# Depthwise convolution of a hybrid decoder: three channel tiles on PE with tables laid out beforehand, two running sums on DVE

## The chip, the cores and the metric

One core of one Trainium2 chip. The metric is the device time of one execution in microseconds (us); lower is better. Of a kernel's runs the median is given.

## The reference

A two-layer decoder trunk over 2048 tokens of 1024 channels, float32. Layer 0 mixes pooling and a state space model. Layer 1, which the change is about, is a gated causal depthwise convolution of width 31, a LayerNorm over channels and an output projection. Cut to that layer:

```python
def _odd_mixer(h, w_in, conv_w, conv_b, ln_g, ln_b, w_out):
    proj = jnp.einsum('bsd,de->bse', h, w_in)
    val, gt, z = ...                      # 1024 channels each
    g = (val * jax.nn.sigmoid(gt)).astype(jnp.float32)
    c = lax.conv_general_dilated(g, conv_w[:, None, :], window_strides=(1,),
        padding=[(30, 0)], feature_group_count=1024) + conv_b
    cc = c - jnp.mean(c, axis=-1, keepdims=True)
    var = jnp.mean(cc * cc, axis=-1, keepdims=True)
    c = cc * lax.rsqrt(var + LN_EPS) * ln_g + ln_b
    y = jax.nn.silu(c) * jax.nn.silu(z)
    return jnp.einsum('bse,ed->bsd', y, w_out)
# x = x + _odd_mixer(_rmsnorm(x), ...); the output is _rmsnorm(x)
```

## The kernel before

The tokens are worked on in two halves of 1024, A and B (`h` = 0 and 1), and each half in two blocks of 512 (`b`). Channels lie in eight tiles `j` of 128. Projections run on PE (TensorE) as three products of split float32 operands, 48 products of 512 columns a unit; a weight is fetched as `raw` and split into a high and a low part `w` by ACT (ScalarE) and DVE (VectorE) ("weight split"; its DVE row is `w<-raw,w`, or `act<-raw,act` for the last four).

Nothing is ordered by hand. Each part of the work is a generator that yields operations; a scheduler (`Sched.run`) merges these streams into one order per engine before anything runs, by estimated engine clocks, and a stream of a lower number (`prio`) goes first among those about as early. Engines then work through their queues in that order. PE's main stream takes the units in this order: layer 0 of A and of B, layer 0's output of A, layer 1's projections of A, layer 0's output of B, layer 1's projections of B, then the output projection of A (`A.q`, eight units `e{eh}t{tp}`: half of the output channels by 256 tokens) and that of B (`B.q`, eight units, all of block 0 first, then block 1).

The projections of layer 1 take, for each channel tile in `ORDER[h]`, gate `g{j}` and value `v{j}`, and then the eight `y{j}`. `post_val` multiplies them and stores the tile to DRAM, for the convolution on DVE into `gd`, for that on PE into `gpd`.

*Convolution on DVE*: `conv_load` brings the tile into a `cg` slot and starts the accumulator `ca` on ACT with tap 0. `conv_thread`, the stream of lowest priority (9), adds the other 30 taps one after the other into that accumulator (`SCALAR_TENSOR_TENSOR ca<-cg,cwt,ca`). The last two tiles go block by block, first both for block 0, then both for block 1. `conv_store` writes the sum to `cd`. *Convolution on PE*: `pe_conv` multiplies tables of shifted taps with eight channels by 16 token phases at a time. `pe_tables` and ACT (with `mask8`) build the tables on the chip. Tiles 6 and 7 (`PEB`) go through PE for both halves together, in products of 128 columns; tiles 4 and 5 only for half B, in products of 64. All of this happens in layer 1 of B. DVE has tiles 0 to 5 of A and 0 to 3 of B.

`ln_thread(h, b)` waits for all eight tiles of `cd` of a block and loads them (`act<-cd`, or `ca<-cd` and `cg<-cd` for B's block 1). It adds them up on DVE to a half sum of 512 columns and lets PE form the mean (`aux<-st,onesN`), subtracts it (`act<-act,aux`), squares on ACT and adds up to a second half sum, lets PE form the variance (`aux<-onesN,st`), takes the inverse root on POOL, spreads it with PE (`aux<-st,ones`) and multiplies. `ln_out` applies gain, SiLU and the gate and splits the result into `y1`, which the output projection reads.

`evac1` empties a finished output unit on DVE, 512 columns twice (`st<-st,mm`); for the second half of the channels, ACT squares, POOL takes a root and DVE multiplies by it and by the norm's gain (`st<-st,sml,act`, here called output norm).

## Time and profile before

| what | us |
|---|---|
| median of 3 runs | 1534.59 (1533.71 to 1536.25) |
| span of the profiled execution | 1533.6 |
| PE busy | 1493.4 |
| DVE busy | 1090.1 |
| ACT busy | 549.5 |
| PE idle in 1400 to 1480 | 3.25 |
| last evacuation of A's output projection, start | 1432.79 |

The profile is of one execution; no other time is given for it than its span, from the first to the last instruction, which lies 1.0 us below the median of the runs. A row of a group reads: line, engine, operation, tile written and tiles read, shape, count, then busy time, mean ns of one, idle time of the engine before it and what ended that. A row of the timeline has start, length and the count of equal instructions that it merges; a row of a window has the length, then the busy time of PE, PEld (weight load), DVE, ACT, POOL, the granted clock, and the DMA's share and GB/s.

### The profile page before, as it was taken

How to read it: one execution, taken by the hardware profiler on the slowest of the kernel's cores; microseconds unless marked ns; L12 is line 12 of the kernel's file. 1: busy time of each engine (PE TensorE's matmuls, PEld its weight loads, DVE VectorE, ACT ScalarE, POOL GpSimd, SP SyncE). 2: the span in 40 equal slices, each digit the busy share in tenths (PEclk: the TensorE clock that was granted, in tenths of full speed). 3: DMA queues.
4: the chain of work that ended last, by engine and by line, in shares of the span. 5: the costliest groups of instructions: out<-in, count | busy, mean ns of one | idle time of the engine just before them, and what ended most of it. 6: DMA issues, size and time to landing. Idle time of an engine off the chain costs nothing. (4 is left out here: it accounts for less than half of the span.)

```text
span 1533.6 us, 18686 instructions
## 1 busy us (share of the span) xinstructions
PE 1493.4 (97%) x7087; PEld 1224.7 (80%) x7087; DVE 1090.1 (71%) x1291; ACT 549.5 (36%) x859; POOL 124.2 (8%) x397
## 2 busy tenths in 40 slices
PE   5999999999999999999999999999999999999997
PEld 4878788888887788888888888888888888887785
DVE  5891567778857323399999999344997898967752
ACT  5322463222134215311111430352354565533431
POOL 4000121000000002000000000120000000003322
PEclk9999999999999999999999999999999999999999
DMA  6227973889665544233353543633466585966753
GB/s 193 83 86 234 313 238 116 255 266 332 221 222 194 168 165 137 83 97 95 98 97 112 191 144 118 218 98 111 88 148 202 160 248 188 354 217 226 246 200 115
DMA packets 248618, 271.35 MB, mean 177 GB/s; under 512 B 58497, under 2 KB 178993, under 8 KB 248528
## 3 DMA queue, kind: packets, MB, share of 16 engines
q1 hardware_dynamic: 248528, 270.15, 55.6%
q8 instruction: 56, 0.92, 0.2%
q14 instruction: 34, 0.28, 0.1%
HBM read 174.49 MB, written 91.42 MB: 173 GB/s over the span
## 5 line engine op out<-in xcount | busy, mean ns | idle before, releaser
L348 PE MATMUL mm<-act,w 128*128 128x512 f32 x4224 | 1004.9, 396 | 0.0
L348 PEld LDWEIGHTS mm<-act,w 128*128 128x128 f32 x4224 | 789.0, 189 | 178.2 <-issue 2.5
L305 DVE SCALAR_TENSOR_TENSOR ca<-cg,cwt,ca 128x1024 f32<-128x1024 f32 (+1 forms) x360 | 397.8, 1106 | 16.1 <-ACT ca L330 5.8
L348 PE MATMUL mm<-w,act 128*128 128x512 f32 x1344 | 316.6, 395 | 1.4 <-DVE w L287 1.4
L348 PEld LDWEIGHTS mm<-w,act 128*128 128x128 f32 x1344 | 251.7, 188 | 60.4 <-DVE w L287 1.8
L287 DVE TENSOR_TENSOR w<-raw,w 128x1024 fp32r<-128x1024 f32 x116 | 141.6, 1222 | 104.3 <-ACT w L319 101.8
L319 ACT CAST w<-raw 128x1024 fp32r<-128x1024 f32 x116 | 121.2, 1045 | 195.6 <-PE mm L348 152.1
L330 ACT ACTIVATE junk<-st 128x1024 bf16<-128x1024 f32 (+1 forms) x64 | 54.0, 844 | 121.3 <-DVE st L287 111.8
L305 DVE SCALAR_TENSOR_TENSOR act<-aux,vcol,act 128x512 fp32r<-128x512 f32 x64 | 45.9, 748 | 66.1 <-ACT act L330 66.0
L287 DVE TENSOR_TENSOR st<-st,mm 128x512 f32<-128x512 f32 x48 | 31.0, 684 | 74.7 <-PE mm L348 74.5
L330 ACT ACTIVATE po<-mm 128x1024 f32<-128x1024 f32 x32 | 32.9, 1027 | 119.8 <-PE mm L348 79.2
L319 ACT CAST act<-st 128x512 fp32r<-128x512 f32 (+1 forms) x64 | 51.8, 860 | 59.1 <-DMA st<-y0d 16.2
L297 POOL TENSOR_SCALAR sml<-sml 128x1 f32<-128x1 f32 (+1 forms) x100 | 34.4, 344 | 430.8 <-ACT junk L330 423.5
L319 ACT COPY st<-aux 128x512 f32<-128x512 f32 (+2 forms) x56 | 25.7, 474 | 114.9 <-PE aux L348 99.7
L330 ACT ACTIVATE act<-act,mask 128x128 f32<-128x128 f32 x192 | 58.0, 390 | 19.4 <-DMA act<-band 19.4
L521 POOL TENSOR_TENSOR sml<-sml,mhalf 128x1 f32<-128x1 f32 (+1 forms) x52 | 34.4, 662 | 346.2 <-DVE sml L295 342.2
L287 DVE TENSOR_TENSOR act<-st,act 128x512 fp32r<-128x512 f32 (+1 forms) x64 | 56.2, 926 | 8.3 <-ACT act L319 8.3
L330 ACT ACTIVATE act<-aux,vcol 128x512 fp32r<-128x512 f32 x64 | 41.6, 686 | 47.6 <-PE aux L362 47.5
L362 PE MATMUL aux<-ident,st 128*128 128x128 f32 (+2 forms) x266 | 38.9, 282 | 20.2 <-DMA st<-in_even_norm 8.7
L330 ACT ACTIVATE st<-mm 128x1024 f32<-128x1024 f32 x24 | 24.6, 1025 | 87.1 <-PE mm L348 84.5
L362 PEld LDWEIGHTS aux<-ident,st 128*128 128x128 f32 (+2 forms) x266 | 32.4, 146 | 28.3 <-POOL sml L297 8.7
L305 DVE SCALAR_TENSOR_TENSOR st<-st,mm 128x1024 f32<-128x1024 f32 x24 | 34.3, 1429 | 23.9 <-PE mm L348 23.9
(146 smaller groups left out, 1001.5 us busy)
## 6 DMA issues: line engine op xcount, KB each, us to landing
raw<-in_odd_w_in SPq DMA_DIRECT2D x48, 512.0 KB
raw<-in_even_w_in SPq DMA_DIRECT2D x32, 512.0 KB
st<-x1d SPq DMA_DIRECT2D x48, 256.0 KB
st<-in_x SPq DMA_DIRECT2D x16, 512.0 KB
raw<-in_even_w_out SPq DMA_DIRECT2D x16, 512.0 KB
z1d<-po SPq DMA_DIRECT2D x16, 512.0 KB
st<-z1d SPq DMA_DIRECT2D x16, 512.0 KB
raw<-in_odd_w_out SPq DMA_DIRECT2D x16, 512.0 KB
```

Of the source, the lines that this page charges most:

```text
L287: return Op("V", d, [a, b], [o], lambda: V.tensor_tensor(o, a, b, op))
L297: e.tensor_scalar(o, a, s1, s2, op0, op1)
L305: return Op("V", d, rd, [o], lambda: V.scalar_tensor_tensor(o, a, s, b, op0, op1))
L319: return Op("A", 0.05 + width(o) / 960.0, [a], [o], lambda: A.copy(o, a))
L330: return Op("A", (0.3 if len(wr) > 1 else 0.13) + width(o) / 960.0, rd, wr, lambda: A.activation(o, a, fn, **kw))
L348: nc.tensor.matmul(o, w, x, start=s, stop=e)
L362: nc.tensor.transpose(o, a, idn)
L521: yield Op("G", 0.3, [a], [o], lambda: G.tensor_tensor(o, a, mhalf[:, :n], ALU.pow))
```

## The change

Tiles 5, 6 and 7 go through PE for both halves, in products of 128 columns, and DVE has tiles 0 to 4 of both halves. `ORDER` of B becomes 0, 1, 5, 6, 7, 2, 3, 4, so the last DVE tile (4) is the eighth of the pairs; before, it was tile 3, the sixth. The tables come as a further input, laid out on the host, and are loaded whole (three times 512 KB for each half of a tile); `pe_tables` and ACT's masking go. The factor 0.5 moves to the bias pass. On DVE a tile has two accumulators: ACT starts them with tap 0 and tap 1, DVE adds even taps to one and odd taps to the other, 29 taps in all, and adds the two at the end. There are four `ca` slots instead of two. Comments and texts in the code are dropped, which moves line numbers: DVE's `tensor_tensor` is line 285 for 287, `scalar_tensor_tensor` 303 for 305, the products 346 for 348.

```diff
 RANK = dict(split=2, pool=4, pec=3, lna=8, lnb=3, y1=3, ssm=4, prep=2)
-PEB = (6, 7)
-PEC = (4, 5) + PEB
-ORDER = (range(NK), (0, 1, 6, 7, 2, 3, 4, 5))
+PEB = (5, 6, 7)
+ORDER = (range(NK), (0, 1, 5, 6, 7, 2, 3, 4))
 
...
     slots("cg", 2, SLOT)
-    slots("ca", 2)
+    slots("ca", 4)
     slots("sml", 12, 16)
     slots("pwt", 1, 256)
-    slots("sml2", 1, 64)
     slots("mm", 3, 1024, psum)
...
     zsw = ctile("zsw", (128, NG))
-    mask8 = ctile("mask8", (128, 8))
-    pch = ctile("pch", (128, len(PEC), 32))
     junk = ctile("junk", (128, 1024), BF16)
...
     Md = [dram(f"Md{i}", (128, 1024)) for i in range(4)]
-    band = [dram(f"band{n}", (128, 768)) for n in range(len(PEC))]
-    gpd = [dram(f"gpd{n}", (128, 16 * (130 if j in PEB else 66))) for n, j in enumerate(PEC)]
-    ctd = [dram(f"ctd{n}", (128, (1 + (j in PEB)) * H)) for n, j in enumerate(PEC)]
+    gpd = [dram(f"gpd{n}", (128, 16 * 130)) for n in range(len(PEB))]
+    ctd = [dram(f"ctd{n}", (128, 2 * H)) for n in range(len(PEB))]
     Kd = [dram(f"Kd{i}", (128, 256)) for i in range(4)]
...
             yield Wait(("cw",))
-            ca = cas[h, j] = yield Alloc("ca")
+            ca, cb = cas[h, j] = yield Alloc("ca", 2)
             yield act(ca[:, :H], gt[:, 0:H], AF.Identity, bias=vc("conv_b", j), scale=cwt[:, j, 0:1])
+            yield act(cb[:, :H], gt[:, 1:H + 1], AF.Copy, scale=cwt[:, j, 1:2])
             done("cg", h, j)
...
             yield Wait(("cg", h, j))
-            gt, ca = cgt[h, j], cas[h, j]
+            gt, (ca, cb) = cgt[h, j], cas[h, j]
             n0, n1 = bl[0] * 512, bl[-1] * 512 + 512
-            acc = ca[:, n0:n1]
-            for k in range(1, NT):
-                yield stt(acc, gt[:, k + n0:k + n1], cwt[:, j, k:k + 1], acc, ALU.mult, ALU.add)
+            acc = ca[:, n0:n1], cb[:, n0:n1]
+            for k in range(2, NT):
+                yield stt(acc[k % 2], gt[:, k + n0:k + n1], cwt[:, j, k:k + 1], acc[k % 2], ALU.mult, ALU.add)
+            yield tt(acc[0], acc[0], acc[1], ALU.add)
             if bl[-1] == 1:
                 free("cg", gt)
+                free("ca", cb)
             spawn(conv_store(h, j, ca, bl), 6, f"cs{h}{j}")
...
 
-    def pe_tables():
-        yield Wait(("cw",))
-        yield Op("V", 0.3, [ident], [mask8], lambda: V.tensor_reduce(
-            out=mask8, in_=ident.rearrange("p (c i) -> p c i", i=16), axis=AX.X, op=ALU.add))
-        for n, j in enumerate(PEC):
-            wp = yield Alloc("sml2")
-            yield gset(wp, 0.0)
-            yield acopy(wp[:, 17:17 + NT], cwt[:, j, :])
-            yield dma(band[n].rearrange("p (j s) -> p j s", j=16),
-                      bass.AP(wp.tensor, wp.offset, [list(wp.ap[0]), [1, 16], [1, 48]]))
-            free("sml2", wp)
-            done("band", n)
     def pe_conv(n, j):
-        halves = (0, 1) if j in PEB else (1,)
-        M = 64 * len(halves)
+        M = 128
         W = M + 2
-        yield Wait(("band", n))
-        for h in halves:
+        for h in range(2):
             yield Wait(("g", h, j))
...
             xt, ot = yield Alloc("st", 2)
-            tz = yield Alloc("act", 4)
-            bt = tz[3]
-            bv = bt[:, 0:384].rearrange("p (g d i) -> p d g i", g=8, d=3)
+            tz = yield Alloc("act", 3)
             xv = xt[:, :8 * W].rearrange("p (g c) -> p g c", g=8)
-            yield dma(bt[:, 0:384].rearrange("p (g s) -> p g s", g=8),
-                      flat(band[n], half * 64 * 768, [[48, 128], [8 * 768, 8], [1, 48]]))
             yield dma(xv, flat(gpd[n], half * 64 * 16 * W, [[W, 128], [8 * 16 * W, 8], [1, W]]))
             for d in range(3):
-                tv = tz[d].rearrange("p (g c i) -> p c g i", g=8, c=8)
-                for c in range(8):
-                    yield act(tv[:, c], bv[:, d], AF.Copy, scale=mask8[:, c:c + 1])
+                yield dma(tz[d], io["conv_t"][n, half, d])
             for q in range(2):
...
             free("st", ot)
-        for i, h in enumerate(halves):
+        for h in range(2):
             it, ot = yield Alloc("st", 2)
             yield dma(it[:, :H].rearrange("p (i m) -> p i m", i=16),
-                      flat(ctd[n], i * 64, [[16 * M, 128], [M, 16], [1, 64]]))
+                      flat(ctd[n], h * 64, [[16 * M, 128], [M, 16], [1, 64]]))
             yield act(ot[:, :H].rearrange("p (m i) -> p i m", i=16)[:, ::-1, :],
-                      it[:, :H].rearrange("p (i m) -> p i m", i=16), AF.Identity, bias=vc("conv_b", j))
+                      it[:, :H].rearrange("p (i m) -> p i m", i=16), AF.Identity, bias=vc("conv_b", j), scale=0.5)
             free("st", it)
...
             t = th[:, :H]
-            if j in PEB or (h == 1 and j in PEC):
-                n = PEC.index(j)
+            if j in PEB:
+                n = PEB.index(j)
                 gp = yield Alloc("st")
-                w0, w = (0, 64) if h == 1 and j in PEB else (2, 66)
+                w0, w = (0, 64) if h == 1 else (2, 66)
                 gv = gp[:, :16 * w].rearrange("p (j c) -> p c j", c=w)
...
             specs.append((f"{p}.v{j}", lambda j=j: job_cols(w_in1, j * 128, f"wv{h}{j}"), post_val(h, j)))
-            if not (j in PEB or (h == 1 and j in PEC)):
+            if j not in PEB:
                 conv_order.append((h, j))
...
     spawn(conv_load(), 6, "convl")
-    spawn(pe_tables(), 7, "pet")
-    for n, j in enumerate(PEC):
+    for n, j in enumerate(PEB):
         spawn(pe_conv(n, j), RANK["pec"], f"pec{j}")
...
         "ssm_b_re", "ssm_b_im", "ssm_c_re", "ssm_c_im", "ssm_d", "ssm_w_glu", "even_w_out",
-        "odd_norm", "odd_w_in", "conv_w", "conv_b", "conv_ln_g", "conv_ln_b", "odd_w_out", "final_norm"]
+        "odd_norm", "odd_w_in", "conv_w", "conv_b", "conv_ln_g", "conv_ln_b", "odd_w_out", "final_norm", "conv_t"]
+def conv_tables(w):
+    t = np.zeros((len(PEB), 2, 3, 8, 16, 8, 8, 16), np.float32)
+    for d in range(3):
+        for j in range(16):
+            for i in range(16):
+                k = j + 16 * d + i - 17
+                if 0 <= k < NT:
+                    for n, tile_ in enumerate(PEB):
+                        v = w[k, tile_ * 128:tile_ * 128 + 128].reshape(2, 8, 8)
+                        for c in range(8):
+                            t[n, :, d, c, j, :, c, i] = v[:, :, c]
+    return t.reshape(len(PEB), 2, 3, 128, 1024)
 
...
 
-    nc = bacc.Bacc("TRN2", target_bir_lowering=False, num_devices=1)
+    nc = bacc.Bacc("TRN2", target_bir_lowering=False, num_devices=1, dynamic_dma_scratch_size=1024)
     arrays, io = {}, {}
     for name in _INS:
-        a = np.ascontiguousarray(inputs[name])
+        a = conv_tables(np.asarray(inputs["conv_w"])[0]) if name == "conv_t" else np.ascontiguousarray(inputs[name])
         arrays[f"in_{name}"] = a
...
     io["out"] = nc.dram_tensor("out", (1, S, D), F32, kind="ExternalOutput").ap()
```

The scheduler then gives another order. PE first, around the end of A's output projection. Before (`mm_1266` is A's last unit, `mm_1281` B's first):

```order
L348 MATMUL mm_1266_10624<-w_1243_10401,act_1186_9976 128x512
L348 MATMUL mm_1266_10624<-w_1242_10400,act_1187_9977 128x512
L348 MATMUL mm_1281_10726<-w_1270_10650,act_1237_10377 128x512
L348 MATMUL mm_1281_10726<-w_1271_10651,act_1237_10377 128x512
L348 MATMUL mm_1281_10726<-w_1270_10650,act_1238_10378 128x512
```

Now (`mm_1226` is A's last unit, `mm_1241` B's first, which reads `act_1269` and `act_1270`, the split of B's first LayerNorm):

```order
L346 MATMUL mm_1226_10209<-w_1201_9968,act_1180_9736 128x512
L346 MATMUL mm_1226_10209<-w_1200_9967,act_1181_9737 128x512
L346 MATMUL aux_1257_10362<-onesN,st_1215_10073 128x1 x4
L346 MATMUL aux_1263_10389<-st_1214_10072,ones_72 128x128 x4
L346 MATMUL mm_1241_10312<-w_1230_10235,act_1269_10415 128x512
L346 MATMUL mm_1241_10312<-w_1231_10236,act_1269_10415 128x512
L346 MATMUL mm_1241_10312<-w_1230_10235,act_1270_10416 128x512
```

Variance and spread of B's first LayerNorm, which stood inside the third and before the fourth unit of A, now stand between the two projections. PE again, between block 0 and block 1 of B's output projection. Before:

```order
L348 MATMUL mm_1321_11010<-act_1308_10891,act_1256_10518 128x512
L348 MATMUL mm_1321_11010<-act_1307_10890,act_1257_10519 128x512
L348 MATMUL mm_1331_11101<-w_1270_10650,act_1315_10957 128x512
L348 MATMUL mm_1331_11101<-w_1271_10651,act_1315_10957 128x512
L348 MATMUL mm_1331_11101<-w_1270_10650,act_1316_10958 128x512
```

Now (`mm_1284` is the last unit of block 0, `mm_1291` the first of block 1):

```order
L346 MATMUL mm_1284_10643<-act_1265_10397,act_1276_10463 128x512
L346 MATMUL mm_1284_10643<-act_1264_10396,act_1277_10464 128x512
L346 MATMUL aux_1305_10787<-st_1302_10780,onesN 128x512
L346 MATMUL aux_1306_10801<-onesN,st_1303_10781 128x1 x4
L346 MATMUL aux_1309_10818<-st_1302_10780,ones_72 128x128 x4
L346 MATMUL mm_1291_10733<-w_1230_10235,act_1312_10833 128x512
L346 MATMUL mm_1291_10733<-w_1231_10236,act_1312_10833 128x512
L346 MATMUL mm_1291_10733<-w_1230_10235,act_1313_10834 128x512
```

All three products of B's second LayerNorm now stand there; before, they stood in A's seventh unit and in B's second. On DVE, the end of the convolution. Before, around its last tap (`ca_1044`; the rows with `mm_1202` and `mm_1206` evacuate A's second and third output unit):

```order
L287 TENSOR_TENSOR st_1203_10094<-st_1203_10094,mm_1202_10093 128x512
L287 TENSOR_TENSOR st_1204_10095<-st_1204_10095,mm_1202_10093 128x512
L287 TENSOR_TENSOR st_1199_10034<-st_1199_10034,st_1198_10033 128x1024
L305 SCALAR_TENSOR_TENSOR ca_1044_8818<-cg_1037_8766,cwt,ca_1044_8818 128x512
L287 TENSOR_TENSOR st_1199_10034<-st_1199_10034,st_1200_10035 128x1024
L287 TENSOR_TENSOR st_1199_10034<-st_1199_10034 128x512
L305 SCALAR_TENSOR_TENSOR ca_1044_8818<-cg_1037_8766,cwt,ca_1044_8818 128x512
L295 TENSOR_SCALAR sml_1210_10219<-aux_1209_10213 128x4
L295 TENSOR_SCALAR st_1198_10033<-ident,sml_1210_10219 128x128 x4
L287 TENSOR_TENSOR st_1207_10166<-st_1207_10166,mm_1206_10165 128x512
```

Now (`mm_1284` is the unit of the fence before last; `ca_1121` and `ca_1122` are the two running sums of tile 4; `st_1302` is the first half sum of B's second LayerNorm):

```order
L285 TENSOR_TENSOR st_1285_10644<-st_1285_10644,mm_1284_10643 128x512
L285 TENSOR_TENSOR st_1286_10645<-st_1286_10645,mm_1284_10643 128x512
L303 SCALAR_TENSOR_TENSOR ca_1121_9284<-cg_1116_9269,cwt,ca_1121_9284 128x512
L303 SCALAR_TENSOR_TENSOR ca_1122_9285<-cg_1116_9269,cwt,ca_1122_9285 128x512
L303 SCALAR_TENSOR_TENSOR ca_1121_9284<-cg_1116_9269,cwt,ca_1121_9284 128x512
L303 SCALAR_TENSOR_TENSOR st_1285_10644<-st_1285_10644,sml_1294_10742,act_1186_9858 128x1024
L303 SCALAR_TENSOR_TENSOR ca_1122_9285<-cg_1116_9269,cwt,ca_1122_9285 128x512
L303 SCALAR_TENSOR_TENSOR st_1286_10645<-st_1286_10645,sml_1295_10745,act_1186_9858 128x1024
L303 SCALAR_TENSOR_TENSOR ca_1121_9284<-cg_1116_9269,cwt,ca_1121_9284 128x512
L285 TENSOR_TENSOR ca_1121_9284<-ca_1121_9284,ca_1122_9285 128x512
L285 TENSOR_TENSOR st_1302_10780<-ca_1298_10772,ca_1299_10773 128x1024
L285 TENSOR_TENSOR st_1302_10780<-st_1302_10780,cg_1300_10774 128x1024
```

The convolution's last sum moved from beside A's second and third output unit to behind the evacuation and the output norms of B's fourth. The first half sum of B's second LayerNorm follows it.

More of the change, by code (lines that the diff above doesn't have):

```diff
@@ L1437, in f @@
                     yield gset(gv[:, 0:2, :], 0.0)
-                elif w0:
-                    yield acopy(gv[:, 0:2, :], pch[:, n, :].rearrange("p (c j) -> p c j", j=16))
-                c0 = 66 - w0 * 33 if h else 0
-                W = 130 if j in PEB else 66
-                yield dma(gpd[n][:, 0:16 * W].rearrange("p (j c) -> p j c", j=16)[:, :, c0:c0 + w],
+                yield dma(gpd[n].rearrange("p (j c) -> p j c", j=16)[:, :, 66 * h:66 * h + w],
                           gp[:, :16 * w].rearrange("p (j c) -> p j c", c=w))
@@ L1447, in f @@
             yield stt(t, t, 1.0, ps, ALU.add, ALU.mult)
-            if h == 0 and j in PEC:
-                yield acopy(pch[:, PEC.index(j), :], t[:, H - 32:H])
             free("mm", ps)
```

## The prediction

> **What bounds the kernel now.** First the page: busy times and the forty slices.
>
> ```profile
> span 1533.6 us, 18686 instructions
> PE 1493.4 (97%) x7087; PEld 1224.7 (80%) x7087; DVE 1090.1 (71%) x1291; ACT 549.5 (36%) x859; POOL 124.2 (8%) x397
> PE   5999999999999999999999999999999999999997
> DVE  5891567778857323399999999344997898967752
> ...
> L348 PE MATMUL mm<-act,w 128*128 128x512 f32 x4224 | 1004.9, 396 | 0.0
> ```
>
> PE is full from the second slice to the last but one; 40.2 us of its span are idle. A projection unit is 48 products of 1004.9/4224 = 0.238 us, 11.4 us in all. So a saving on another engine is worth nothing by itself, and a late result that PE must wait for costs its whole length. Then the stages, by windows (length, PE, PEld, DVE, ACT, POOL busy, clock):
>
> ```profile
> 1070.00:1370.00 300.00, 299.16 (x1510) 251.02 (x1509) 262.44 (x278) 149.27 (x299) 6.28 (x15) 1.00 0.65 195
> 1400.00:1440.00 40.00, 37.83 (x161) 29.73 (x159) 29.80 (x29) 13.82 (x22) 19.16 (x47) 1.00 0.58 191
> 1440.00:1480.00 40.00, 38.92 (x176) 31.76 (x177) 29.15 (x34) 18.30 (x30) 9.58 (x24) 1.00 0.71 239
> ```
>
> In layer 1 of half B (1070 to 1370) PE waits for 0.84 us in 300, while DVE is 87% busy: the second engine to run out there. The depthwise convolution on DVE is the work of lowest priority (9), so it gets what the rest leaves.
>
> **The change, part by part.** PE first, groups by shape, with two of ACT; the last line is one weight load of 512 KB in the chain of waits:
>
> ```profile
> L348 PE MATMUL aux<-st,act 128*128 128x128 f32 x192 | 23.0, 275 | 0.8 <-ACT act L330 0.8
> L348 PE MATMUL aux<-st,act 128*128 128x64 f32 x192 | 22.3, 273 | 0.0
> L330 ACT ACTIVATE act<-act,mask 128x128 f32<-128x128 f32 x192 | 58.0, 390 | 19.4 <-DMA act<-band 19.4
> L330 ACT ACTIVATE ca<-cg,vcol,cwt 128x1024 f32<-128x1024 f32 x10 | 12.5, 1245 | 27.3 <-DMA cg<-gd 19.3 <-DMA cd<-ca 8.0
> ...
> 1440.59 3.79 DMA raw<-in_odd_w_out
> ```
>
> A product of 64 columns takes as long as one of 128. The two half tiles (192 records, 22.3 us) go, one whole tile (96 records, half of 23.0, 11.5 us) comes: PE loses **10.8 us**, all on its own path. The 58.0 us of masking go from ACT, which is 36% busy; PE waited 0.8 us in all for it, so I give this 0. The 18 table loads of 512 KB that replace it need nothing computed, only three act slots, and run beside PE's units of 11.4 us; a load that lost this cover would cost its 3.79 us. Ends 0 and 8 (two exposed); I take 0. On SP's queue the 18 issues replace 12 of the old tables (four stores, eight loads). The second running sum's start adds ten ACT passes like the 12.5 us of the first, beside work that PE does anyway: 0. Half A's sixth tile leaves DVE, in a stage where PE waits for nothing: 0, the time stays PE's.
>
> DVE's convolution, two groups by shape, then the timeline (start, length of a run of equal instructions):
>
> ```profile
> L305 DVE SCALAR_TENSOR_TENSOR ca<-cg,cwt,ca 128x1024 f32<-128x1024 f32 x240 | 307.8, 1284 | 8.9 <-ACT ca L330 1.9
> L305 DVE SCALAR_TENSOR_TENSOR ca<-cg,cwt,ca 128x512 f32<-128x512 f32 x120 | 90.0, 751 | 7.2 <-ACT ca L330 3.9
> ...
> 937.40 7.88 DVE L305 SCALAR_TENSOR_TENSOR ca<-cg,cwt,ca 128x1024 f32<-128x1024 f32 x6
> 1179.54 11.77 DVE L305 SCALAR_TENSOR_TENSOR ca<-cg,cwt,ca 128x512 f32<-128x512 f32 x15
> 597.99 1.41 DVE L305 SCALAR_TENSOR_TENSOR act<-aux,vcol,act 128x512 fp32r<-128x512 f32 x2
> ```
>
> One of 512 lasts 0.75 us. In the chain, 15 take 11.77: a pitch of (11.77-0.75)/14 = 0.787, with a gap. Two independent ones of the same form take 1.41, a pitch of 0.66: they overlap. So two alternating sums should step at about 0.67 for 512 and 0.12 less than (7.88-1.28)/5 = 1.32, that is 1.20, for 1024. Ends: no gain (1.32) and this (1.20); I take 1.20, the row of the same operation.
>
> The Trainium skill says otherwise (VectorE: DVE Perf Modes, "The DRAIN you can't avoid"): after each Vector operation the pipe empties before the next starts, and leaving out waits does not help. By that sentence alone two sums would gain nothing; the trace does not agree, the pair above took 1.41 us where two of 0.75 in a row would take 1.50.
>
> What DVE has to do in B: four tiles before (two of 30 x 1.32, two of 60 x 0.787) are 173.6 us. Now five: three of 29 x 1.20 + 1.22 and two of 58 x 0.67 + 1.4, 188.6 us. That is 15 us more, and later: the last DVE tile is now the eighth of B's channel pairs, not the sixth, four projections or about 46 us of PE time. The 87% leave little room, so convolution steps of lowest priority spill far behind. The orders show how far. PE's last block of B (second 512 tokens) needs B's second LayerNorm, which needs the last convolution sum. In the new order on DVE it stands after the evacuation of B's fourth output unit, and in PE's order the LayerNorm's three products stand alone between the units. Nothing is left on PE to hide them. The first LayerNorm of B likewise ends only after A's last unit. Two gaps on PE, priced from these rows (DVE and SP timeline):
>
> ```profile
> 1347.58 1.29 DVE L287 TENSOR_TENSOR st<-st,mm 128x512 f32<-128x512 f32 x2 [1.80 <-PE mm L348]
> 1350.04 0.69 DVE L287 TENSOR_TENSOR st<-st 128x512 f32<-128x512 f32 x1
> 1352.63 4.62 DVE L287 TENSOR_TENSOR act<-act,aux 128x1024 f32<-128x1024 f32 x4 [0.45 <-PE aux L348]
> 1364.10 0.69 DVE L287 TENSOR_TENSOR st<-st 128x512 f32<-128x512 f32 x1
> 1364.71 0.74 DVE L305 SCALAR_TENSOR_TENSOR ca<-cg,cwt,ca 128x512 f32<-128x512 f32 x1
> 1365.48 0.32 SPq L339 DMA_DIRECT2D cd<-ca  x1
> 1368.26 0.53 SPq L339 DMA_DIRECT2D ca<-cd  x1
> 1426.56 1.22 DVE L287 TENSOR_TENSOR w<-raw,w 128x1024 fp32r<-128x1024 f32 x1
> 1432.79 1.28 DVE L287 TENSOR_TENSOR st<-st,mm 128x512 f32<-128x512 f32 x2
> 1444.44 0.68 DVE L287 TENSOR_TENSOR st<-st 128x512 f32<-128x512 f32 x1
> 1452.98 2.36 DVE L287 TENSOR_TENSOR ca<-ca,st 128x1024 f32<-128x1024 f32 x2
> 1457.20 1.23 DVE L287 TENSOR_TENSOR act<-raw,act 128x1024 fp32r<-128x1024 f32 x1 [0.73 <-ACT act L319]
> 1463.25 3.49 DVE L287 TENSOR_TENSOR act<-st,act 128x1024 fp32r<-128x1024 f32 x3
> 1479.20 1.29 DVE L287 TENSOR_TENSOR st<-st,mm 128x512 f32<-128x512 f32 x2 [0.87 <-PE mm L348]
> 1486.11 1.28 DVE L305 SCALAR_TENSOR_TENSOR st<-st,sml,act 128x1024 f32<-128x1024 f32 x1 [1.81 <-POOL sml L285]
> 1501.50 1.28 DVE L287 TENSOR_TENSOR st<-st,mm 128x512 f32<-128x512 f32 x2 [9.86 <-PE mm L348]
> ```
>
> The last tap of the convolution ended at 1365.45 before, between A's second and third output unit. Rows "st<-st,mm ... x2" are evacuations of a finished output unit: the first of A at 1347.58, A's last at 1432.79, B's fourth at 1479.20, its sixth at 1501.50. An undisturbed unit takes (1501.50-1479.20)/2 = 11.15 us.
>
> *Gap 1*, counted from the evacuation of A's last unit, which PE's end releases. The new DVE order then has both output norms (the second starts 6.91 after the evacuation, 1479.20 to 1486.11, and ends at 8.2), a weight split (1.2), then the LayerNorm's half sum. From a half sum to the first multiplication by the inverse deviation took 8.54 at its shortest (1444.44 to 1452.98). Then three multiplications, a weight split, three products and the first split of the result, eight at (3.49-1.22)/2 = 1.14: 9.1. Together 27.0. A second path: the eight weight splits of B's projection, spaced by their loads over 30.64 us before (1426.56 to 1457.20, eight of them), stand in the same queue, the first some 6 us ahead of that evacuation: the eighth at +24.6, and 5 to 6 us of products and split after it, +30. I take **30**; ends 25 and 34.
>
> *Gap 2*, from the evacuation of B's fourth unit. Both norms 8.2, the last tap and the sum of the two accumulators 1.4: 9.6. Store to the load that waits for it 2.8 (1365.48 to 1368.26); three loads in flight, one took 3.79, I take 6: 18.4. One add 1.2, half sum; to the subtraction 2.6 (1350.04 to 1352.63): 22.2. To the next half sum 11.5 (1352.63 to 1364.10), less 2.0 for the other work in between: 31.7. To the multiplication 8.5: 40.2. To the end of the first split 11.5 with other work (1452.98 to 1464.4), about 7 without: 47. PE then catches up with the third pair of channels, 2: **49**; ends 41 and 56.
>
> Two credits and a cost. From 1347.58 to 1432.79 seven units took 85.2 instead of 78.1, to 1479.20 four took 46.4 instead of 44.6: 8.9 us of LayerNorm products and short waits, of which all but one batch (0.8) now lie in the gaps: minus **8.1**. And a gap costs clock (windows; the column after POOL is the clock):
>
> ```profile
> 500.00:504.00 4.00, 2.28 (x10) 1.50 (x8) 3.59 (x4) 1.33 (x2) 0.00 (x0) 1.00 0.46 147
> 504.00:508.00 4.00, 3.42 (x14) 2.88 (x15) 1.91 (x3) 1.52 (x4) 0.00 (x0) 0.61 0.40 137
> ```
>
> After about 2.3 us of idling the next 4 us ran at 0.61: 1.7 us, twice **3.4**.
>
> Sum: 1533.6 - 10.8 + 30 + 49 - 8.1 + 3.4 = 1597.1 for the span; the median of the runs stands 1.0 above the profiled span: **1598 us**, 4.1% slower.
>
> **Rivals.** (1) *Two sums step like one*: 1.32 and 0.787 stay. Between the evacuations of the gaps' neighbours stand up to 15 taps, 11.8 us against a unit of 11.15, so DVE itself falls behind by about 2 us in each of three units, less what the three PSUM slots hide: about 1603. For it: every run of taps in this trace steps so; against it: the pair at 1.41. The Trainium skill's sentence above would have it so. (2) *Faster: both LayerNorms of B stay hidden.* It needs DVE to be ahead of PE by a unit at A's end, so that gap 1 and gap 2 are empty; then only PE's 10.8 us remain: 1524. It decides where the last sum is done before B's second unit ends. For it: DVE gets 0.12 us per tap back; against it: an in-order queue cannot pass an evacuation that waits for PE, and the sum stands behind one. (3) *The gaps are half as long* because the loads and ACT's parts run beside the norms: 25 + 30 instead of 79, 1574. For it: my chain adds measured pieces that had other work in them; against it: the norms' 8.2 and the 8.5 are shortest values. (4) *More waits upstream*: DVE at capacity also delays A's LayerNorm or a weight split, PE waits in 1180 to 1350 as well, some 15 us: 1613. For it: 87%; against it: PE waited 0.84 us there at that load, and these have priority over taps.
>
> **How the numbers follow.** Forecast 0.66, rival 1 0.12, rival 2 0.05, rival 3 0.08, rival 4 0.09. The gaps' ends give 1598 - 13 and + 11; with rivals 1 and 4 and part of 3 the range is 1580 to 1614. A difference below 0.2% is no more than a measurement of this kernel can tell from none. Faster only rival 2: 0.05; the same needs gaps that just cancel 19 us: 0.02; slower 0.93.
>
> **What would show it.** In the changed profile: PE idle near 115 us instead of 40; two idle stretches of PE after about 1410, one of some 30 and one of some 50 us, ended by DVE's splits of y1; the chain that ended last running through DVE, POOL and the load of the convolution sums instead of PE alone; taps at a pitch near 1.20 and 0.67; PE's f32 products of 128 columns 288 times and about 34.5 us. Wrong if PE has no gap above 10 us there, or if the taps' sum ends before A's last unit.

## The result and the profile after

The changed kernel takes **1606.51 us** (median of 4 runs, 1603.25 to 1608.93), the kernel before 1535.42 (4 runs, 1533.71 to 1537.45): ratio 1.0451, 95% interval 1.0428 to 1.0474. It is slower by 71 us, where 63 were predicted. The page of the changed kernel (span, busy times, slices):

```profile
span 1604.3 us, 18290 instructions
PE 1492.9 (93%) x6991; PEld 1219.7 (76%) x6991; DVE 1066.0 (66%) x1290; ACT 502.5 (31%) x665; POOL 128.3 (8%) x393
PE   5999999999999999999999999999999999958357
DVE  5881667878766223799998822459718888779562
PEclk9999999999999999999999999999999999978769
```

PE idles for 1604.3 - 1492.9 = 111.4 us, 40.2 before, and almost all of the new idling lies in the slices from the 36th on. PE's busy time is that of before (1493.4), though 96 products are gone. The convolution's products take 10.0 us less (35.3 for 45.3), but from A's first output unit on PE is busy for 9.0 us more (193.3 for 184.3). About half of that is the products of B's two LayerNorms, 11.0 us for 6.2: they now stand alone in gaps, in which the granted clock was 0.55 in the mean. Also new in DVE's row are the 2s of the 24th and 25th slice (where A's sixth tile was) and the 1 of the 30th (1163 to 1203).

PE's timeline there (start, length; in brackets the idle time ahead and what ended it):

```profile
1402.09 18.70 PE L346 MATMUL mm<-w,act 128*128 128x512 f32 x78
1435.72 1.87 PE L346 MATMUL aux<-onesN,st 128*128 128x1 f32 x8 [14.94 <-DVE st L285]
1440.95 2.04 PE L346 MATMUL aux<-st,ones 128*128 128x128 f32 x8 [3.36 <-DVE st L293]
1451.19 1.22 PE L346 MATMUL mm<-w,act 128*128 128x512 f32 x2 [8.19 <-ACT act L317]
1452.88 23.03 PE L346 MATMUL mm<-w,act 128*128 128x512 f32 x94 [0.47 <-DVE act L285]
1475.75 22.14 PE L346 MATMUL mm<-act,act 128*128 128x512 f32 x96
1522.94 2.04 PE L346 MATMUL aux<-st,onesN 128*128 128x512 f32 x2 [25.05 <-DVE st L285]
1534.30 1.83 PE L346 MATMUL aux<-onesN,st 128*128 128x1 f32 x8 [9.32 <-DVE st L285]
1539.02 2.04 PE L346 MATMUL aux<-st,ones 128*128 128x128 f32 x8 [2.88 <-DVE st L293]
1546.89 1.22 PE L346 MATMUL mm<-w,act 128*128 128x512 f32 x2 [5.83 <-ACT act L317]
1548.36 7.03 PE L346 MATMUL mm<-w,act 128*128 128x512 f32 x24 [0.24 <-DVE act L285]
```

There are the two gaps: from 1420.8 (the end of A's last unit) to 1451.2, with variance and spread of B's first LayerNorm standing alone in it, and from 1497.9 to 1546.9, with all three products of the second. Each ends with ACT's part of the split of `y1` (L317); DVE's part, which alone the prediction had named, holds PE up for another 0.47 and 0.24 us.

DVE's timeline at the second gap:

```profile
1499.73 1.28 DVE L285 TENSOR_TENSOR st<-st,mm 128x512 f32<-128x512 f32 x2
1509.23 0.75 DVE L303 SCALAR_TENSOR_TENSOR ca<-cg,cwt,ca 128x512 f32<-128x512 f32 x1
1510.01 0.69 DVE L285 TENSOR_TENSOR ca<-ca,ca 128x512 f32<-128x512 f32 x1
1517.38 1.22 DVE L285 TENSOR_TENSOR st<-ca,ca 128x1024 f32<-128x1024 f32 x1 [6.68 <-DMA ca<-cd]
1533.46 0.69 DVE L285 TENSOR_TENSOR st<-st 128x512 f32<-128x512 f32 x1
1541.72 2.36 DVE L285 TENSOR_TENSOR ca<-ca,st 128x1024 f32<-128x1024 f32 x2 [2.26 <-ACT st L317]
```

The last tap of the convolution starts at 1509.23, 9.5 us behind the evacuation of B's fourth output unit; it ended at 1365.45 before. Then come the store, the loads (6.68 us of waiting), and the chain of the LayerNorm. And here DVE had lost time earlier (window 1150 to 1210: length, PE, PEld, DVE, ACT, POOL, clock):

```profile
1150.00:1210.00 60.00, 59.23 (x329) 50.87 (x329) 12.80 (x11) 17.75 (x17) 0.00 (x0) 1.00 0.93 255
```

DVE worked for 12.80 of these 60 us: it had finished tile 1 of B at 1157, and tile 2, which came behind the pairs of the three PE tiles, was there at 1207. PE had its own work and hardly waited (59.23 of 60), so nothing in PE's row tells that 47 us of DVE are lost there. That they are what is missed 300 us later is an argument so far; the runs with another order of the pairs, below, bear it out.

### The profile page after: what moved, and what is told of

It reads as the page before. It is cut to its first block, busy times and chain, and to the rows that moved or that the text cites. A ratio compares the mean times of both kernels' runs of the same rounds, so it can differ in the third digit from the quotient of the medians.

```text
span 1604.3 us, 18290 instructions
## 1 busy us (share of the span) xinstructions
PE 1492.9 (93%) x6991; PEld 1219.7 (76%) x6991; DVE 1066.0 (66%) x1290; ACT 502.5 (31%) x665; POOL 128.3 (8%) x393
## 5 line engine op out<-in xcount | busy, mean ns | idle before, releaser
L303 DVE SCALAR_TENSOR_TENSOR ca<-cg,cwt,ca 128x1024 f32<-128x1024 f32 (+1 forms) x348 | 361.1, 1101 | 7.9 <-ACT ca L328 7.9
L317 ACT CAST w<-raw 128x1024 fp32r<-128x1024 f32 x116 | 121.2, 1045 | 206.1 <-PE mm L346 168.0
L317 ACT COPY st<-aux 128x512 f32<-128x512 f32 (+2 forms) x52 | 25.1, 499 | 159.4 <-PE aux L346 141.2
L317 ACT CAST act<-st 128x512 fp32r<-128x512 f32 (+1 forms) x64 | 51.6, 855 | 52.0 <-DMA st<-yd 16.1
L328 ACT ACTIVATE po<-mm 128x1024 f32<-128x1024 f32 x32 | 32.8, 1024 | 103.8 <-issue 52.6
L516 POOL TENSOR_TENSOR sml<-sml,mhalf 128x1 f32<-128x1 f32 (+1 forms) x52 | 38.0, 731 | 317.3 <-DVE sml L293 313.3
L285 DVE TENSOR_TENSOR po<-po,mm 128x1024 f32<-128x1024 f32 x8 | 9.8, 1222 | 57.9 <-PE mm L346 57.9
```

Source lines behind the costliest of these rows:

```text
L285: return Op("V", d, [a, b], [o], lambda: V.tensor_tensor(o, a, b, op))
L303: return Op("V", d, rd, [o], lambda: V.scalar_tensor_tensor(o, a, s, b, op0, op1))
L317: return Op("A", 0.05 + width(o) / 960.0, [a], [o], lambda: A.copy(o, a))
L328: return Op("A", (0.3 if len(wr) > 1 else 0.13) + width(o) / 960.0, rd, wr, lambda: A.activation(o, a, fn, **kw))
L516: yield Op("G", 0.3, [a], [o], lambda: G.tensor_tensor(o, a, mhalf[:, :n], ALU.pow))
```

## The experiments

**Tables and sums without the tile split.**

```diff
-PEB = (5, 6, 7)
-ORDER = (range(NK), (0, 1, 5, 6, 7, 2, 3, 4))
+PEB = (6, 7)
+PEC = (4, 5, 6, 7)              # 4 and 5 for half B only, products of 64 columns
+ORDER = (range(NK), (0, 1, 6, 7, 2, 3, 4, 5))
```

> The change without its tile split: PE has tiles 6 and 7 whole and 4 and 5 for half B, in before's order of B, but the tables come by DMA and DVE has two running sums with four slots. Theory (tables and sums move nothing that PE waits for): 1535, ends 1530 and 1538. Rival (18 to 24 loads of tables are exposed): 1542 or more. Rival (DVE's 22 us less in half B are worth something): 1528 or less.

Measured: 1536.98 us, ratio 1.0001 (0.9984 to 1.0019). The theory holds: table loads and second sum together move nothing; the whole loss comes with the tile split and the order of B's pairs that belongs to it.

**One running sum.**

```diff
-            ca, cb = cas[h, j] = yield Alloc("ca", 2)
+            ca = cas[h, j] = yield Alloc("ca")
...
-            for k in range(2, NT):
-                yield stt(acc[k % 2], ..., acc[k % 2], ALU.mult, ALU.add)
-            yield tt(acc[0], acc[0], acc[1], ALU.add)
+            for k in range(1, NT):
+                yield stt(acc, ..., acc, ALU.mult, ALU.add)
```

> The changed kernel with one running sum again (30 taps, one accumulator of the pair; four slots kept). The order of PE's instructions is the same. Theory: steps go back to 1.32 and 0.787 us; where 9 to 15 taps stand between two evacuations of A's and B's output units DVE falls behind by 1 to 2 us each, and the last sum comes later: +5 to +20, 1618. Rival (the second sum gives nothing): 1606, steps of 1.20 and 0.66 or no effect on the end. Rival (the second sum is itself the cost, by ACT's pass and the slots): faster, 1590.

Measured: 1606.53 us, ratio 1.0439 (1.0417 to 1.0461): no effect on the end, and the theory's +5 to +20 is refuted. The steps did change. Runs of taps, first two of the changed kernel, then the same two with one sum and its last two taps:

```profile
1122.55 14.43 DVE L303 SCALAR_TENSOR_TENSOR ca<-cg,cwt,ca 128x1024 f32<-128x1024 f32 x12
1477.15 8.70 DVE L303 SCALAR_TENSOR_TENSOR ca<-cg,cwt,ca 128x512 f32<-128x512 f32 x13
```

```profile
1118.45 15.81 DVE L303 SCALAR_TENSOR_TENSOR ca<-cg,cwt,ca 128x1024 f32<-128x1024 f32 x12
1475.15 10.20 DVE L303 SCALAR_TENSOR_TENSOR ca<-cg,cwt,ca 128x512 f32<-128x512 f32 x13
1508.56 1.53 DVE L303 SCALAR_TENSOR_TENSOR ca<-cg,cwt,ca 128x512 f32<-128x512 f32 x2
```

The pitches are (14.43 - 1.28)/11 = 1.20 and (8.70 - 0.75)/12 = 0.66 with two sums, 1.32 and 0.79 with one. But in a row of 13 taps between two evacuations the slower step only uses up time in which DVE would wait for PE's unit, and the taps before 1157 only shorten the idling. The last two taps stand at 1508.56 to 1510.09 here; in the changed kernel the last tap and the sum behind it end at 1510.70. So at this place DVE's queue follows PE: a tap that stands behind an evacuation waits for PE, however fast it is.

**The last tile's taps cut.**

```diff
-            for k in range(2, NT):
+            for k in range(2, 4 if (h, j) == (1, 4) else NT):
```

> Leaves out all taps but 0 to 3 of tile 4 in half B (54 steps of 0.66 us, 36 us of DVE). The orders of PE and DVE are made anew: B's LayerNorm of block 0 now stands inside A's fourth to sixth output units, that of block 1 still alone after B's fourth. Theory: gap 1 (27.9) goes, gap 2 (48.6) stays, since block 1 of tile 3 is still of lowest priority and stands behind B's evacuations: 1606.5 - 27.9 - 2 = 1577, ends 1565 and 1590. Rival (amount of DVE work alone): both gaps go, 1525. Rival (neither): 1606.

Measured: 1569.72 us, ratio 1.0195 (1.0176 to 1.0214), 7 us under the theory's value. PE's timeline:

```profile
1441.41 18.65 PE L346 MATMUL mm<-w,act 128*128 128x512 f32 x71 [7.01 <-DVE w L285]
1459.89 22.27 PE L346 MATMUL mm<-act,act 128*128 128x512 f32 x96
1498.96 1.84 PE L346 MATMUL aux<-onesN,st 128*128 128x1 f32 x8 [13.34 <-DVE st L285]
1511.57 1.22 PE L346 MATMUL mm<-w,act 128*128 128x512 f32 x2 [5.83 <-ACT act L317]
```

Gap 1 is gone, but for 7.01 us of a weight split. Gap 2 stays where the order puts it, with the same four steps (two of them in the fence), shortened to 1511.6 - 1482.2 = 29.4, since the last sum was ready before the unit ended. That the 37 us equal the 36 us of cut steps looks like an engine that paces the end; the runs below show that it is not so simple.

**Another order of the pairs, twice.**

```diff
-ORDER = (range(NK), (0, 1, 5, 6, 7, 2, 3, 4))
+ORDER = (range(NK), (0, 1, 5, 2, 6, 3, 7, 4))    # first run
+ORDER = (range(NK), (0, 1, 5, 6, 2, 3, 4, 7))    # second run
```

> Half B takes the tiles in the order 0, 1, 5, 2, 6, 3, 7, 4: PE's tiles stand between DVE's, so tile 2 reaches DVE two pairs earlier and tile 3 one; tile 4 stays last. In the order the LayerNorm products of B, block 0 stand inside A's second output unit and those of block 1 inside B's first and third, none alone. Theory (late DVE work puts the last sum behind PE): the gaps of 27.9 and 48.6 us and the products at a low clock between them go, 1606.5 - 76.5 - 5 = 1525, ends 1520 and 1540 (new waits in front of A's first unit). Rival (the amount of DVE work, one tile more, sets it): PE still waits about 75 us somewhere after 1300, 1590 to 1606. Rival (tables from DRAM or the second sum cost the time): 1600.

> Half B in the order 0, 1, 5, 6, 2, 3, 4, 7: all DVE tiles after the second one pair (22.7 us) earlier. In the order both LayerNorms of B stand inside A's first to fifth output units, but those of A stand alone, four groups of products between the last projection and A's first output unit. Theory: the two gaps after 1410 go (-76.5, -5 of clock), and one new gap opens in front of A's first unit, where the half sum waits for its inverse (8.5), the store and load of y1 (about 8) and its splits (about 10): 27. 1606.5 - 81.5 + 27 = 1552, ends 1530 and 1570. Rival (amount of DVE work): 1590 or more.

Measured: 1580.95 us, ratio 1.0272 (1.0252 to 1.0293), and 1601.07 us, ratio 1.0397 (1.0371 to 1.0422). Both theories' values (1525, 1552) are missed. Of the first run, then of the second, PE's timeline:

```profile
1371.77 1.84 PE L346 MATMUL aux<-onesN,st 128*128 128x1 f32 x8 [13.99 <-DVE st L285]
1394.57 1.22 PE L346 MATMUL mm<-w,act 128*128 128x512 f32 x2 [15.60 <-ACT act L317]
```

```profile
1351.14 0.79 PE L346 MATMUL aux<-st,ones 128*128 128x128 f32 x2 [15.08 <-DVE st L293]
1367.54 1.22 PE L346 MATMUL mm<-w,act 128*128 128x512 f32 x2 [15.60 <-ACT act L317]
1419.26 8.32 PE L346 MATMUL mm<-w,act 128*128 128x512 f32 x24 [15.96 <-ACT act L317]
```

The two gaps after 1410 are gone, as the theory said. In their place PE waits for the LayerNorms of **A**: in the first run in front of A's third output unit, in the second in front of the first and the third. A PE tile is convolved for both halves together, so A's LayerNorm waits until the last PE tile's pair of B has been through PE. The pairs that come early for the sake of A's LayerNorm are those that keep DVE's tiles of B back. The first run's theory had only one side of this; the second's had one gap of 27 us in front of A's first unit, where PE in fact had only the LayerNorms' products from 1325.5 to 1367.5, and none in front of the third.

On DVE's side the first run answers the question left open above. Its window and the sum behind its last tap:

```profile
1150.00:1210.00 60.00, 59.17 (x305) 49.85 (x305) 54.69 (x51) 14.35 (x14) 0.00 (x0) 1.00 0.85 208
1446.91 0.69 DVE L285 TENSOR_TENSOR ca<-ca,ca 128x512 f32<-128x512 f32 x1
```

With the same work as the changed kernel, and nothing but the order edited, DVE was busy for 54.69 of the 60 us instead of 12.80, and its last sum came 63 us earlier.

**PE's tiles for half B alone.**

```diff
-PEB = (5, 6, 7)
+PEB = ()
+PEC = (5, 6, 7)                 # half B only; A's eight tiles all on DVE
-ORDER = (range(NK), (0, 1, 5, 6, 7, 2, 3, 4))
+ORDER = range(NK), range(NK)
```

> PE convolves tiles 5, 6 and 7 for half B alone (288 products of 64 columns), half A has all eight tiles on DVE, B's order is 0 to 7; tables and two sums as in the changed kernel, the planner's estimates as they were. A's LayerNorm no longer waits for pairs of B, and DVE need not idle for tile 2 (56 us between 1151 and 1207 in the changed kernel). In the order B's LayerNorm of block 0 stands inside A's fourth to sixth output units, that of block 1 alone after B's fourth. Theory (DVE paces the end, a microsecond of its work or idling moves the end by one, as the cut taps did): 1606.5 - 56 = 1550, ends 1540 and 1570. Rival (the place in PE's order alone decides: gap 1 goes, gap 2 stays whole): 1606.5 - 30.6 = 1576. Rival (the fifth tile's 37 us come on top, and A's tiles 5 to 7 run past 1060): 1590 or more. Rival (no gap is left): 1525.

Measured: 1599.45 us, ratio 1.0418 (1.04 to 1.0435): near the rival in which A's tiles run past 1060, and A's last tile did end at 1095. The picture of the second rival is there too: gap 1 is gone and gap 2 is whole (62.1 us between the first products of B's fourth and fifth unit, 60.2 in the changed kernel), but most of what gap 1 gave is lost again elsewhere. DVE was busy for 52.4 of the 60 us from 1150 to 1210, and still its last sum came only at 1503.20 (below): it has A's tiles 5 to 7 to do as well. That is not the whole reason, though, as the next run shows, which has the same tiles, B's order 0, 1, 6, 7, 2, 3, 4, 5, and these lines:

```diff
+            if name.startswith(("B.g",)):
+                rate[0] = 2176.0           # the planner's estimate of a product, columns a us; 2400 until then
...
-    spawn(ln_thread(1, 0, y1[1]), RANK["lnb"], "lnB0")
+    spawn(after((y1[0].name, 7, 1), ln_thread(1, 0, y1[1])), RANK["lnb"], "lnB0")
```

> As the run before, B's order 0, 1, 6, 7, 2, 3, 4, 5, B's LayerNorm not before A's y1 is split, and the planner's estimate of a product at the measured 0.238 us from layer 1 of B on only, so that layer 0 keeps its order. All LayerNorm products stand inside units, B's block 1 in A's last unit and B's second and third. Theory (DVE paces the end): about as the run before, 1550, ends 1535 and 1565, only with many short waits of PE instead of one gap. Rival (place in the order decides): no gap, 1526. Rival (the estimate itself harms, also in layer 1): 1575 or more.

Measured: 1563.44 us, ratio 1.0176 (1.0155 to 1.0198), at the upper end of the theory's range. ("B.g" is also the start of the names of layer 0's last projections of B, so the estimate changed a little earlier than the expectation says.) DVE, from 1060 to 1340 and from 1340 to 1500, then the sum of the two accumulators behind the last tap; first without, then with the new estimate:

```profile
1060.00:1340.00 280.00, 280.00 (x1363) 234.11 (x1362) 254.12 (x240) 87.03 (x99) 5.58 (x10) 0.99 0.63 207
1340.00:1500.00 160.00, 137.60 (x587) 109.98 (x586) 123.66 (x154) 44.82 (x79) 37.45 (x89) 0.95 0.55 187
1503.20 0.69 DVE L286 TENSOR_TENSOR ca<-ca,ca 128x512 f32<-128x512 f32 x1
```

```profile
1060.00:1340.00 280.00, 277.76 (x1358) 231.37 (x1357) 268.20 (x271) 84.62 (x97) 5.55 (x10) 0.99 0.60 198
1340.00:1500.00 160.00, 148.67 (x637) 118.74 (x636) 123.39 (x144) 59.24 (x93) 31.15 (x76) 0.97 0.63 217
1426.26 0.68 DVE L286 TENSOR_TENSOR ca<-ca,ca 128x512 f32<-128x512 f32 x1
```

By 1340 DVE had done 14 us more in the second, and after it as much; but its last sum came 77 us earlier, and the kernel is 36 us faster. Both have the same convolution work on DVE, so it is not the amount alone but the place of the taps in the queue. What moved them is not shown: the estimate, the order of the pairs and the gate all differ between these two runs. An explanation by the estimate would be this: the planner takes a product to last 0.216 us where it lasts 0.238, thinks that a unit leaves DVE a microsecond less than it does, and puts taps of the lowest priority behind evacuations that come much later than it thinks.

**The estimate for the whole program**, in the kernel before, in the changed one, and with PE's tiles for half B alone:

```diff
-        d = sum(width(o) / 2400.0 if x.dtype == F32R else ...
+        d = sum(width(o) / 2176.0 if x.dtype == F32R else ...
```

> The kernel before with the planner's estimate of a product at the measured 0.238 us; nothing else. In the order B's LayerNorm of block 1 moves from A's seventh to B's second unit up to A's third to fifth. Theory: PE waited for neither of them, so the time stays, 1535, ends 1530 and 1538. Rival (the estimate is a gain of its own): 1525 or less. Rival (DVE's work is pushed ahead of weight splits and evacuations): 1540 or more.

> The changed kernel; only the planner's estimate of a product goes from 0.216 us (512/2400 + 0.0027) to the measured 0.238 (512/2176 + 0.0027), so that it leaves DVE more time per unit of PE. Same work. In the new order B's LayerNorm of block 0 stands inside A's fourth to sixth output units, that of block 1 still alone after B's fourth. Theory (the order, made with PE estimated too fast, sets the taps too late): gap 1 (27.9) goes, gap 2 (48) stays: 1606.5 - 28 - 3 = 1575, ends 1565 and 1590. Rival (the amount of DVE work and the arrival of tile 2 set it, the order only follows): no gain, the gap moves in front of A's units, 1600 or more.

> PE convolves tiles 5, 6 and 7 for half B alone (products of 64 columns, 288 of them, tables by DMA as in the changed kernel); half A has all eight tiles on DVE, where DVE was idle between 904 and 1060 us; B's order is 6, 0, 7, 1, 2, 3, 4, 5; two sums; the planner's estimate of a product is the measured 0.238 us. In the order all LayerNorm products stand inside units, B's block 1 in A's last and B's second and third. Theory (place, not amount: A's tile 5 and A's LayerNorm no longer wait for B's pairs, B's tile 2 comes earlier): no gap; PE has 33.5 us of convolution products for 45.3 before: 1535.4 - 11.8 = 1524, ends 1518 and 1540. Rival (amount: five tiles of B, 188 us, and what is left of A's after 1060 are more than DVE can do by 1450): one gap of 30 to 50 us, 1555 to 1575.

Measured: 1615.87 us, ratio 1.0505 (1.0483 to 1.0527); 1639.14 us, ratio 1.0649 (1.0625 to 1.0672); 1595.5 us, ratio 1.0371 (1.0343 to 1.0399). All three theories fail. What they have in common I had not thought of: the order of layer 0 changes as well. Layer 1 of B begins 53 us later than in the kernel before in the first run, 29 us later than in the changed kernel in the second, and at 1063.6 in the third. That is the second run's whole loss (33 us in the medians, 28 in the profiled executions), but 53 of 82 us in the first. The window up to 650 of the first run, then that of the kernel before:

```profile
0.00:650.00 650.00, 598.26 (x2911) 485.44 (x2912) 384.36 (x611) 221.26 (x318) 56.23 (x204) 0.98 0.59 191
```

```profile
0.00:650.00 650.00, 623.63 (x3075) 510.96 (x3076) 393.41 (x623) 231.80 (x332) 58.85 (x211) 0.99 0.61 195
```

25 us of PE's busy time are missing there before the convolution begins, and more is lost at later stages. The shorter estimate seems to be of use there, perhaps since it lets the planner prepare things early; that was not looked into. These runs say nothing on the tile split. What the estimate did in the changed kernel after layer 0 stays open: gap 1 went, but as much waiting came up elsewhere.

**Additions on POOL.** Half-B tiles as above in the order 0 to 7, late estimate but no gate for B's LayerNorm, and A's LayerNorm additions moved:

```diff
+        eng = G if h == 0 else None
-        yield tt(sm, cc[0], cc[1], ALU.add)
+        yield tt(sm, cc[0], cc[1], ALU.add, eng)
...
-        yield tt(s, s, c, ALU.mult)
+        yield tt(s, s, c, ALU.mult, G if out is None else None)
```

> As the run before with B's order 0 to 7, and the additions of A's two LayerNorms and the multiplication of its gate on POOL instead of DVE: 12 adds and 8 multiplications of 1.2 us and 4 half sums of 0.7 leave DVE, 27 us, all after about 1060. Theory (DVE paces the end): 1550 - 27 = 1523, not below PE's own 1525, ends 1522 and 1545. Rival (POOL's additions hold DVE up as long as they run, or A's LayerNorm now comes late): 1550 or more.

Measured: 1600.1 us, ratio 1.0416 (1.04 to 1.0431): the rival. An addition of 1024 takes POOL 3.3 us, A's LayerNorm comes late (PE waited 24.2 us for POOL's sums), and DVE's taps get slower beside it. A group of POOL, a run of seven taps on DVE, two single taps out of it, and POOL's additions in the same time:

```profile
L284 POOL TENSOR_TENSOR st<-st,act 128x1024 f32<-128x1024 f32 x12 | 39.7, 3329 | 16.2 <-ACT act L329 14.5 <-DMA st<-z1d 1.4
1089.33 15.89 DVE L304 SCALAR_TENSOR_TENSOR ca<-cg,cwt,ca 128x1024 f32<-128x1024 f32 x7
1092.92 3.42 DVE L304 SCALAR_TENSOR_TENSOR ca<-cg,cwt,ca 128x1024 f32<-128x1024 f32 x1
1096.26 3.43 DVE L304 SCALAR_TENSOR_TENSOR ca<-cg,cwt,ca 128x1024 f32<-128x1024 f32 x1
1092.29 2.97 POOL L284 TENSOR_TENSOR st<-act,act 128x1024 f32<-128x1024 f32 x1 [51.68 <-DMA act<-cd]
1095.33 3.27 POOL L284 TENSOR_TENSOR st<-st,act 128x1024 f32<-128x1024 f32 x1
```

The first three taps of the run, before POOL begins, step at 1.20 us. The other four each last until about 1.08 us after an addition of POOL has ended (1096.34 after 1095.26, 1099.69 after 1098.60). (The order of the pairs and the gate differ from the run with 1563.44 us too, so how much of the loss is POOL's wasn't separated.)

**One whole tile, two for half B.** A's tiles 5 and 6 on DVE, where it has room; tile 7 for both halves:

```diff
-PEB = (5, 6, 7)
-ORDER = (range(NK), (0, 1, 5, 6, 7, 2, 3, 4))
+PEB = (7,)
+PEC = (5, 6, 7)
+ORDER = (range(NK), (0, 1, 7, 2, 3, 4, 5, 6))
...
+            if name.startswith(tuple(f"B.g{j}" for j in range(8))):
+                rate[0] = 2176.0
```

(with the gate of the half-B run above).

> PE convolves tile 7 for both halves and tiles 5 and 6 for half B alone, B's order is 0, 1, 7, 2, 3, 4, 5, 6; DVE has seven tiles of A and five of B; the planner's estimate of a product is 0.238 us from the first gate of layer 1 of B on (in the run e10 it began already at layer 0's output of B). A's tiles 5 and 6 ended at 1014 there, before B's first tile is ready at 1060, and only A's tile 7 (1022 to 1084) ran over. In the order all LayerNorm products stand inside units, B's block 1 after A's seventh and inside B's second. Theory (work that DVE still has after 1060 paces the end, given an order that doesn't push the taps behind the evacuations): e10 minus the 24 us that tile 7 took after 1060, 1563 - 24 = 1539, ends 1528 and 1555. Rival (PE's own limit is reached): 1525, faster than before. Rival (A's LayerNorm, which waits for pair 7 again, opens a gap in front of A's output units): 1565 or more.

Measured: 1553.31 us, ratio 1.0099 (1.008 to 1.0118), inside the theory's range, at its upper end.

```profile
PE   5999999999999999999999999999999999999997
1424.96 1.23 DVE L286 TENSOR_TENSOR st<-ca,ca 128x1024 f32<-128x1024 f32 x1 [5.32 <-DMA ca<-cd]
```

PE shows no gap, and the first addition of B's last LayerNorm is at 1424.96 instead of 1517.38. It is the fastest of the kernels with three tiles on PE, 53 us faster than the changed one, and still 1% slower than the kernel before. PE's products of the convolution take 36.0 us instead of 45.3, but the saving goes into many short waits: in layer 1 of B PE is idle for 9.4 us instead of 0.8. Counting its products of 512 columns back from the end: layer 1 of B begins 8.9 us later than before (3.8 of it are there already at 522 us, before the convolution begins; DVE has A's tiles 5 and 6 to do in the stage before it, which was not shown to be the cause of the rest), lasts 321.6 us instead of 318.8, and from A's first output unit to the last product it takes 198.0 instead of 188.4. No kernel that was run beats the one before.

## Why the prediction was right, step by step

The forecast was 1598 (1580 to 1614). The same count of products cuts the difference of the two profiled executions into pieces; the last column is what the prediction had for it.

| piece | before | after | difference | predicted |
|---|---|---|---|---|
| start to layer 1 of B | 1017.5 | 1020.7 | +3.2 | 0 |
| layer 1 of B | 318.8 | 309.8 | -9.0 | -10.8 |
| A's first to last output unit | 83.1 | 79.0 | -4.1 | part of -8.1 |
| to B's first (gap 1) | 11.1 | 41.7 | +30.6 | +30 |
| B's first to fourth | 37.4 | 35.5 | -1.9 | part of -8.1 and +3.4 |
| to B's fifth (gap 2) | 11.1 | 60.2 | +49.1 | +49 |
| B's fifth to last | 33.4 | 36.5 | +3.1 | part of +3.4 |
| sum, to the end of the last product | | | +70.9 | +63.5 |

The sum came out 7.4 us higher than predicted: 3.2 from the start, 1.8 from layer 1 of B, 0.7 from the gaps and 1.8 from credits and clock.

*Saving on PE.* The row of the conv products has 288 of them, as said, in 35.3 us for 34.5:

```profile
L346 PE MATMUL aux<-st,act 128*128 128x128 f32 x288 | 35.3, 276 | 1.9 <-DMA act<-in_conv_t 1.9
```

The 18 table loads cost 1.9 us of waiting (ends 0 and 8, taken as 0), and the 0.8 us of waiting for the masks are gone: 35.3 - 45.3 + 1.9 - 0.8 is the -9.0, but for 0.1. *Start.* The +3.2 are there already at 521.2 us (517.9 before), while the convolution, the first work that the change touches, begins at 654; in the six executions with the changed tables and layer 0 as it was (the changed kernel, the run without the tile split, and those with one sum, with the taps cut and with the two other orders) layer 1 of B begins between 1016.3 and 1022.1, so this is scatter of single executions.

*Gaps.* Right to 0.7 us in sum, by steps that err in both directions. In gap 2, counted from the evacuation at 1499.73: taps and sum ended at 11.0 (predicted 9.6), the first addition stood at 17.7 (18.4), the second half sum at 33.7 (31.7), the multiplication at 42.0 (40.2), PE's first product at 47.2, and it ran on from 48.6 (47 and 49). In gap 1 the half sum came at 11.7 (9.4) behind the evacuation at 1423.32, the multiplication 8.7 later (8.54), PE's run at 29.6 (30). The weight splits, the second path, ended at 25.0, in time. So the 30 was partly luck: it was taken from the weight splits, but the chain of the LayerNorm held PE up, and that had been put at 27.0. It was 2.3 short at its first step, the two output norms, which were read behind B's fourth unit (8.2). The rows shown in the prediction had the step itself: behind A's last evacuation at 1432.79 the half sum came at 1444.44, that is at 11.65.

*Credits and clock.* These were mis-sized: -8.1 and +3.4 were predicted, -4.7 in sum; measured were -4.1, -1.9 and +3.1, that is -2.9. A's units still ran at 79.0/7 = 11.29 instead of 11.15, though PE was busy all the time (79.00 of 79.00 us). Of the +3.1 PE was idle for 1.0, in short waits. The clock (windows of 4 us, the column after POOL) cost 4 x 0.36 = 1.4 us behind gap 1 and 4 x 0.44 = 1.8 behind gap 2, one window each, for 1.7 taken (4 x 0.39 from the prediction's own row is 1.6):

```profile
1452.00:1456.00 4.00, 3.53 (x11) 2.52 (x11) 4.00 (x4) 1.03 (x2) 0.00 (x0) 0.64 0.21 66
1547.00:1551.00 4.00, 3.76 (x9) 2.57 (x10) 4.00 (x5) 1.31 (x2) 0.00 (x0) 0.56 0.26 72
1551.00:1555.00 4.00, 4.00 (x18) 2.93 (x16) 3.30 (x4) 3.65 (x6) 0.00 (x0) 1.00 0.00 0
```

The Trainium skill (TensorE: Matmul & The Clock Gate, The HAM clock gate and HAM oscillation) says that an idle gap over some 3.4 us puts PE back to half its clock until it has been busy as long. For these gaps the trace agrees: 0.50 inside the first one (1426 to 1435), 0.64 and 0.56 in the first windows behind them and 1.00 after. The prediction's row from the kernel before goes further than the page: there 0.61 followed on only 2.29 us of idling.

*Rivals.* (1) Two sums that step like one: refuted by the pitches of 1.20 and 0.66, and worth nothing at the end anyway by the run with one sum. By the Trainium skill's sentence set beside this rival in the prediction (VectorE: DVE Perf Modes, The DRAIN you can't avoid) the pitch could not have fallen below 1.28 and 0.75; for two alternating sums the trace does not agree with that sentence alone. The same section adds, which the prediction left out, that a next operation which is not held starts earlier, and with that the pitches agree. (2) Faster: no run got there. (3) Gaps half as long: no, they came out whole, +30.6 and +49.1. (4) Waits upstream: PE was busy for 278.1 of the 280 us from 1060 to 1340, so no. The chain that ended last was of no use as evidence: it reaches back only to 1550 in this profile.

Where the reasons were incomplete: the prediction put the lateness down to 15 us more work and the later last tile. The window at 1150 shows 47 us in which DVE had nothing to do, three times as much, and the first run with another order, which filled most of them, had its last sum 63 us earlier. The runs show two more things that the prediction lacked: A's LayerNorm hangs on the same pairs, and with the same work on DVE the last sum can come 77 us earlier or later by the order alone that the planner makes. How much of that goes with its estimates was not separated.

## What to carry to other kernels

When work moves from a full engine to one with spare time, ask when that engine has the time and whether the input is there by then: an average share of 71% hid that half A had the room and half B did not. Where a planner or a list fixes in-order queues, work of lowest priority behind an instruction that waits for another engine runs at that engine's pace, and making it faster can be worth nothing (1606.5 us with one sum as with two). An estimate in a planner that is wrong by 10% may be what a good order rests on (correcting it for the whole program cost the kernel before 5%): correct it for one stage at a time, and look at all the others.

## What the runs showed of the hardware

An independent pair of running sums overlaps on DVE: 1.20 us a step for 1024 columns and 0.66 for 512, where an instruction lasts 1.28 and 0.75; taps on one sum step at 1.32 and 0.79. And POOL slows DVE down: with its additions running beside, taps stepped at 1096.26 - 1092.92 = 3.34 us instead of 1.20, about the length of one addition (3.27), though the expectation had that only as a rival. The Trainium skill (Trainium Architecture — The Big Picture, What this means for kernel authors) says that DVE and GpSimd contend for one shared pair of ports, by an exclusive lock. The trace agrees as far as it goes: each tap beside POOL ended about 1.08 us behind an addition, as if it had stood still until then.
